# Attention beside a paged decode: key sums one step later behind GpSimd's products, a fifth key buffer, and the queries' low part on all 128 rows

## The chip, the cores and the metric

The kernel runs on one core of one Trainium2 chip. The core has a matrix engine (TensorE, PE in the profile, with its weight loads as PEld), three engines for elementwise work (VectorE as DVE, ScalarE as ACT, GpSimd as POOL), and a queue that issues the transfers (SyncE, SP or SPq). The metric is the device time of one execution in microseconds; the median of several runs counts.

## The reference

One inference step of a two-layer trunk runs for a prompt of 1024 tokens and for 8 samples of one token each, with a past of 4096 tokens in pages. The first layer holds stick-breaking attention (8 heads of 64) beside a pooling branch; the second is a convolution module. Cut to what the change touches:

```python
def stick_breaking(q, k, v, q_pos, k_pos, sb_bias):
    z = jnp.einsum('bqhd,bkhd->bhqk', q, k) / math.sqrt(SB_HEAD_DIM) + sb_bias[None, :, None, None]
    causal = k_pos[None, :] < q_pos[:, None]
    log_keep = jnp.where(causal, jax.nn.log_sigmoid(-z), 0.0)
    after = lax.cumsum(log_keep, axis=3, reverse=True) - log_keep
    w = jnp.where(causal, jnp.exp(jax.nn.log_sigmoid(z) + after), 0.0)
    return jnp.einsum('bhqk,bkhd->bqhd', w, v)

# the pooling branch, windows w of 2, 4, 8 and 16 tokens, one per group of 128 columns
        diffs.append((hi - lo) / count[None, :, None] - uf[:, POOL_STATE:, c0:c1])
    y = jnp.einsum('btgc,gcd->btgd', jnp.stack(diffs, axis=2), w_pool) * pool_scale
```

For the samples, q has one row and k and v are 4096 past rows, gathered by a page table. All values are float32. The kernel splits each operand of a large product into a high part that the matrix engine takes in its float32r format and a low part, the rest, and sums the partial products.

## The kernel before

The program is written in one order, and each engine and the DMA queue keep the order in which their instructions are written. The first layer's projection is cut into blocks of 128 output columns, each over three chunks of 384, 384 and 264 tokens. A generator, `blocks_gen`, writes it piece by piece (24 matmuls per chunk, L225 to L227), so that attention can be written between the pieces. Weights arrive as `wraw`; ACT writes the high part `whi` (L205), GpSimd the low part `wlo` (L210).

Attention runs over 48 units: four pairs of heads, eight query blocks of 128 rows, and for query blocks 4 to 7 two pieces of keys. Per pair there are thus four units of 256 columns (the widths 128 and 256, padded to 256), two of 384 and six of 512. For a unit, `z_a` writes the scores into two PSUM tiles, one per head: a full-array matmul each from the queries' high part `sq` (tile qh) and the keys `km`, then a matmul each on 64 rows from the low part `ql`, and, in a query block's first piece, a mask through identb and maskb (L823). `stick_a` forms the two sigmoids on ACT (L360, L361), `z_b` the running product by a scan (L365) and the weights `sg` (L369, L371) on DVE. `tpart` transposes the weights one unit later (L845), and `ppart` multiplies them with the values (L861). `prep` makes the two query parts for the next 256 query rows, in 16 calls: ACT copies the high part, DVE subtracts for the low part (L794), and copies on the DMA queue put each head's high part on both halves of the rows (L796, and L797 two points later).

Beside this runs `decode_k`, the samples' scores. Attention lets it make a certain number of steps per unit (`tick`), 2.3 to 3.8 by its width. In each step it loads two pages of keys into a buffer of 512 KB (`kt`, tag kv, L405), multiplies the pages loaded two steps earlier with the query row (L417; 7 of 8 on GpSimd, the eighth on DVE), and sums a product over the 64 columns of each head on DVE (L409). The steps left over when attention ends go one by one into the output projection's groups (L1029 to L1031), in which DVE also makes some weights' low parts.

The pooling branch, `evac_u`, takes a chunk of the projection out of PSUM: ACT copies it to `u`, DVE forms the window sum in `cur` (L694 or the scan L697) and from it `hb` (L705). Later `g2` multiplies hb with a weight (L713), scales it, gates it on GpSimd (L715) and stores it.

Of the kernel before, what the change touches and what calls it, by code (L numbers as in the profile page):

```python
# [14 lines left out]
F32 = mybir.dt.float32  # L15
# [49 lines left out]
KBUF = 4  # L65
# [35 lines left out]
def kernel(  # L101
# [75 lines left out]
    def defer(n, fn):  # L177
        deferred.append([n, fn])
# [210 lines left out]
    def decode_k():  # L389
        qrow = {0: query_rows(0)}  # L390
        yield
        for hf in range(2):
# [5 lines left out]
            for s in range(len(units) + KLAG + 1):  # L398
                if s < len(units):
                    bi, j = units[s]  # L400
                    if j % 4 == 0:
                        pg = page_ids(hf * 4 + bi, j, 4)
                    kt = dk.tile([P, 2, HW], F32, tag="kv", name="kt", bufs=KBUF)
                    for i in range(2):
                        sp.dma_start(kt[:, i, :], ck[ds(pg[j % 4 + i], 1)].rearrange("o t f -> t (o f)"))  # L405
                    kts[s] = kt
                if s >= KLAG + 1:
                    bi, j = units[s - KLAG - 1]
                    dve.tensor_reduce(out=seg[:, j // 8, j % 8:j % 8 + 2, bi * 8:bi * 8 + 8],  # L409
                                      in_=kts.pop(s - KLAG - 1).rearrange("p a (h d) -> p a h d", d=DH),  # L410
                                      op=ALU.add, axis=AX.X)
                if KLAG <= s < len(units) + KLAG:
                    bi, j = units[s - KLAG]
                    b = hf * 4 + bi
                    kt = kts[s - KLAG]
                    eng = gp if (j // 2) % KMOD < KPOOL else dve
                    eng.tensor_tensor(out=kt, in0=kt, in1=qrow[b], op=ALU.mult)  # L417
                    if j == NPG - 6 and b < NB - 1:
                        qrow[b + 1] = query_rows(b + 1)
                yield  # L420
# [255 lines left out]
    def evac_u(g):  # L676
# [3 lines left out]
        def f(c, c0, n, o):  # L680
# [11 lines left out]
            cur = ab.tile([P, 16 + CMAX], F32, tag="us", name="us", bufs=2)  # L692
            if g == 0:
                dve.tensor_tensor(out=cur[:, 16:16 + m], in0=o[:, 0:m], in1=u[:, 15:15 + m], op=ALU.add)  # L694
            else:
                prev = state["cur"][:, 15 + CMAX:16 + CMAX] if c else 0.0
                dve.tensor_tensor_scan(out=cur[:, 16:16 + m], data0=o[:, 0:m], data1=u[:, 16 - w:16 + m - w],  # L697
                                       initial=prev, op0=ALU.add, op1=ALU.subtract)
            state["cur"] = cur
            hb = ab.tile([P, CMAX], F32, tag="hbt", name="hbt", bufs=2)  # L700
            if c == 2:
                dve.tensor_tensor(out=cur[:, 16 + m:16 + n], in0=o[:, m:n], in1=spool[:, g, :],
                                  op=ALU.add)
            s0 = 0 if c else w - 1
            dve.scalar_tensor_tensor(out=hb[:, s0:n], in0=cur[:, 16 + s0:16 + n], scalar=1.0 / w,  # L705
                                     in1=o[:, s0:n], op0=ALU.mult, op1=ALU.subtract)
            if c == 0:
                gp.tensor_tensor(out=hb[:, 0:w - 1], in0=cur[:, 16:16 + w - 1], in1=rcnt[:, 0:w - 1], op=ALU.mult)
# [80 lines left out]
    def prep(pair, i):  # L789
        q = QO[:, pair, i * 256:(i + 1) * 256]  # L790
        sq = ab.tile([P, 2, 256], F32R, tag="qh", name="qh", bufs=2)
        ql = ab.tile([P, 256], F32R, tag="ql", name="ql", bufs=2)
        act.activation(out=sq[:, 0], in_=q, func=AF.Copy)
        dve.tensor_tensor(out=ql, in0=q, in1=sq[:, 0].bitcast(F32), op=ALU.subtract)  # L794
        for r in (slice(0, DH), slice(DH, P)):
            sp.dma_start(sq[r, 1].bitcast(F32), sq[DH:P, 0].bitcast(F32))  # L796
        defer(2, lambda: sp.dma_start(sq[DH:P, 0].bitcast(F32), sq[0:DH, 0].bitcast(F32)))  # L797
        SQ[pair, i] = sq, ql
# [7 lines left out]
    def z_a(u):  # L806
# [4 lines left out]
        sq, ql = SQ[pair, qb // 2]  # L811
# [4 lines left out]
        for hh in range(2):  # L816
            r = slice(hh * DH, hh * DH + DH)
            pe.matmul(zs[hh][:, 0:nz], ql[r, qs], km[r, hh, c0:c0 + nz], start=False, stop=not first)
# [865 lines left out]
```

## Time and profile before

| | |
|---|---|
| median of 3 runs | 1142.12 us (1140.06 to 1147.91) |
| the profiled execution | 1143.3 us |
| its span in the profile | 1141.5 us |
| PE, PEld busy | 1051.7 us (92%), 841.7 us (74%) |
| DVE, ACT, POOL busy | 812.6 us (71%), 491.9 us (43%), 665.1 us (58%) |
| granted TensorE clock, mean | 0.971 |

The profile's span is 1.8 us shorter than the execution's own time. The busy shares are means over stages with different limits; attention lies between about 70 and 500 us.

### The profile page before, as it was taken

The page shows a single profiled execution, that of the slowest core. Times are in us where ns is not written, and L with a number is a line of the kernel's source. Part 1 is how long each engine was busy: PE and PEld are TensorE (multiplying, and loading weights), DVE is VectorE, ACT ScalarE, POOL GpSimd, SP SyncE. Part 2 cuts the span into 40 slices and gives each one's busy share as a digit, 9 for nine tenths or more (in the row PEclk, how much of TensorE's full clock was granted, in tenths as well). Part 3 has the DMA queues.
Part 4 walks back from the last instruction along what each step waited for, and adds up shares of the span by engine and source line. Part 5 has one row for each costly group of instructions (what it writes and reads, how often), then busy time and mean ns, then how long its engine had stood idle before and what let it go on. Part 6 is the DMA issues. An engine that isn't in the chain of part 4 may idle for free.

```text
span 1141.5 us, 19830 instructions
## 1 busy us (share of the span) xinstructions
PE 1051.7 (92%) x6804; PEld 841.7 (74%) x6804; DVE 812.6 (71%) x961; ACT 491.9 (43%) x929; POOL 665.1 (58%) x502
## 2 busy tenths in 40 slices
PE   8998888889999998797998999999999999899994
PEld 7897777768877877697997666566666466677784
DVE  3458878688599898767348399999999960484246
ACT  4345465547565565571204224444544422462210
POOL 3277879691788889872418336765766612343235
PEclk9999999999999999898999999999999999899997
DMA  8577767783467976655203887787687678386922
GB/s 267 170 230 231 243 194 222 207 251 98 141 217 219 278 216 216 199 194 203 68 26 142 240 253 249 234 252 217 194 266 236 210 237 264 122 280 218 322 102 113
DMA packets 179206, 235.20 MB, mean 206 GB/s; under 512 B 15418, under 2 KB 95939, under 8 KB 179081
## 3 DMA queue, kind: packets, MB, share of 16 engines
q1 hardware_dynamic: 179105, 233.94, 65.1%
q8 instruction: 53, 0.87, 0.3%
q14 instruction: 48, 0.39, 0.1%
HBM read 212.60 MB, written 16.14 MB: 200 GB/s over the span
## 4 chain that ended last, share of the span: by engine, by line
PE 54%; POOL 13%; DVE 11%; issue 9%; DMA 7%; ACT 3%; SPq 3%; POOLq 0%; DVEq 0%; ACTq 0%
PE acc L225 11%; PE acc L227 10%; PE acc L226 10%; POOL kt L417 7%; PE qv L1151 5%; DMA kt<-in_cache_k_dram 3%; DVE zw L409 3%; PE acc L1029 3%; POOL wlo L210 2%; PE acc L1031 2%; PE acc L1030 2%; DVE kp L365 2%; DMA vt<-in_cache_v_dram 1%; DVE xl L196 1%; POOL xres L1021 1%
## 5 line engine op out<-in xcount | busy, mean ns | idle before, releaser
L225 PE MATMUL acc<-xh,whi 128*128 128x384 f32 (+2 forms) x960 | 361.5, 377 | 11.5 <-DVE hbt L705 5.7
L227 PE MATMUL acc<-xl,whi 128*128 128x384 f32 (+2 forms) x960 | 340.4, 355 | 0.2 <-DVE xl L196 0.2
L226 PE MATMUL acc<-xh,wlo 128*128 128x384 f32 (+2 forms) x960 | 339.7, 354 | 0.0
L417 POOL TENSOR_TENSOR kt<-kt,qbs 128x1024 f32<-128x1024 f32 x112 | 274.1, 2464 | 39.6 <-DMA kt<-in_cache_k_dram 30.0
L210 POOL TENSOR_TENSOR wlo<-wraw,whi 128x512 fp32r<-128x512 f32 x122 | 161.6, 1328 | 184.1 <-ACT whi L205 179.5
L1373 DVE SCALAR_TENSOR_TENSOR conv_acc<-hbuf,wdwT,conv_acc 128x1024 f32<-128x1024 f32 x196 | 252.8, 1290 | 6.8
L225 PEld LDWEIGHTS acc<-xh,whi 128*128 128x128 f32 x960 | 184.3, 192 | 78.1 <-issue 26.1
L409 DVE TENSOR_REDUCE zw<-kt 128x16 f32<-128x1024 f32 x128 | 153.6, 1212 | 63.5 <-POOL kt L417 63.3
L227 PEld LDWEIGHTS acc<-xl,whi 128*128 128x128 f32 x960 | 184.3, 192 | 18.0 <-DVE xl L196 0.7
L226 PEld LDWEIGHTS acc<-xh,wlo 128*128 128x128 f32 x960 | 185.0, 193 | 15.7 <-issue 0.3
L1363 POOL TENSOR_TENSOR conv<-conv,tap 128x512 f32<-128x512 f32 x84 | 105.9, 1293 | 17.6 <-ACT tap L1360 17.6
L1029 PE MATMUL acc<-whi,xh 128*128 128x256 f32 x352 | 102.4, 291 | 0.0
L1031 PE MATMUL acc<-whi,xl 128*128 128x256 f32 x352 | 99.5, 283 | 2.1 <-DVE xl L196 2.1
L1030 PE MATMUL acc<-wlo,xh 128*128 128x256 f32 x352 | 99.4, 282 | 0.0
L365 DVE TENSOR_TENSOR_SCAN kp<-kp,zt 128x512 f32<-128x512 f32 (+3 forms) x96 | 92.4, 963 | 1.2 <-ACT zt L361 1.2
L205 ACT ACTIVATE whi<-wraw 128x512 fp32r<-128x512 f32 x126 | 77.4, 624 | 32.1 <-DMA wraw<-in_w_out_ab_dram 14.1
L360 ACT ACTIVATE kp<-zt,nbiash 128x512 f32<-128x512 f32 (+3 forms) x96 | 55.8, 581 | 71.4 <-DVE sg L371 40.7
L1360 ACT ACTIVATE tap<-hbuf,wdwT 128x512 f32<-128x512 f32 x84 | 59.7, 721 | 48.0 <-POOL conv L1363 38.1
L1151 PE MATMUL qv<-vt,zw 128*32 128x512 f32 x512 | 76.1, 604 | 3.1 <-DMA vt<-in_cache_v_dram 3.1
L1029 PEld LDWEIGHTS acc<-whi,xh 128*128 128x128 f32 x352 | 66.8, 190 | 7.9 <-issue 7.4
L1031 PEld LDWEIGHTS acc<-whi,xl 128*128 128x128 f32 x352 | 67.0, 190 | 2.3 <-DVE xl L196 2.3
L845 PE MATMUL zt<-ident,sg 128*128 128x128 f32 x288 | 44.7, 286 | 24.2 <-DVE sg L371 12.9
(274 smaller groups left out, 1507.3 us busy)
## 6 DMA issues: line engine op xcount, KB each, us to landing
kt<-in_cache_k_dram SPq DMA_DIRECT2D x256, 256.0 KB
vt<-in_cache_v_dram SPq DMA_DIRECT2D x256, 256.0 KB
wraw<-in_w_in_c_dram SPq DMA_DIRECT2D x48, 256.0 KB
vt<-in_w_in_c_dram SPq DMA_DIRECT2D x48, 256.0 KB
wraw<-in_w_in_ab_dram SPq DMA_DIRECT2D x46, 256.0 KB
xt<-in_x_prompt_dram SPq DMA_DIRECT2D x8, 512.0 KB
wraw<-in_w_out_ab_dram SPq DMA_DIRECT2D x16, 256.0 KB
xres<-in_x_prompt_dram SPq DMA_DIRECT2D x8, 512.0 KB
```

What stands on the lines that cost most here:

```text
L210: (eng or gp).tensor_tensor(out=lo, in0=raw, in1=hi.bitcast(F32), op=ALU.subtract)
L225: pe.matmul(o, hi[:, k % 4, :], xh, start=(k == 0), stop=False)
L226: pe.matmul(o, lo[:, k % 4, :], xh, start=False, stop=False)
L227: pe.matmul(o, hi[:, k % 4, :], xl, start=False, stop=(k == NK - 1))
L365: dve.tensor_tensor_scan(out=kr, data0=kr, data1=z[:, 0:1].broadcast_to([P, n]), initial=1.0 if prev is None else prev, op0=ALU.mult, op1= ...
L409: dve.tensor_reduce(out=seg[:, j // 8, j % 8:j % 8 + 2, bi * 8:bi * 8 + 8], in_=kts.pop(s - KLAG - 1).rearrange("p a (h d) -> p a h d", d=DH),
L417: eng.tensor_tensor(out=kt, in0=kt, in1=qrow[b], op=ALU.mult)
L1029: pe.matmul(o, XH[:, k, cs], hi[:, k % 2, :], start=(k == 0), stop=False)
L1030: pe.matmul(o, XH[:, k, cs], lo[:, k % 2, :], start=False, stop=False)
L1031: pe.matmul(o, XL[:, k, cs], hi[:, k % 2, :], start=False, stop=(k == NK - 1))
L1151: pe.matmul(pv[32 * bi:32 * bi + 32, :], Z[:, j % 8 * 4 + j // 8, :], vts[bi], start=(j == 0), stop=(j == NPG - 1), tile_position=(0, 32 * ...
L1373: dve.scalar_tensor_tensor(out=part[1], in0=hb[:, j:j + S], scalar=w, in1=part[1], op0=ALU.mult, op1=ALU.add)
```

## The change

The number of key buffers goes from four to five, and a key sum stands two steps behind its product instead of one. The low part of the queries gets a second plane (`sl`) and is copied to both halves of the rows as the high part is, so that its score matmuls take 128 rows, and the four matmuls of a unit alternate between the two PSUM tiles in pairs. The window sum of the pooling branch is written into hb directly; the tile `us` shrinks to the one column that the next chunk's scan starts from.

```diff
--- before.py
+++ after.py
@@ -62,7 +62,7 @@
 TAT = 2
 WLEAD = 2
 G2LAG = 5
-KBUF = 4
+KBUF = 5
 WRB = 3
 ETICK = 0.35
 EDVE = (1, 2, 3, 0)
@@ -395,7 +395,7 @@
             seg = Z.rearrange("p (g s) r -> p s g r", s=4)
             units = [(bi, j) for bi in range(4) for j in range(0, NPG, 2)]
             kts = {}
-            for s in range(len(units) + KLAG + 1):
+            for s in range(len(units) + KLAG + 2):
                 if s < len(units):
                     bi, j = units[s]
                     if j % 4 == 0:
@@ -404,10 +404,10 @@
                     for i in range(2):
                         sp.dma_start(kt[:, i, :], ck[ds(pg[j % 4 + i], 1)].rearrange("o t f -> t (o f)"))
                     kts[s] = kt
-                if s >= KLAG + 1:
-                    bi, j = units[s - KLAG - 1]
+                if s >= KLAG + 2:
+                    bi, j = units[s - KLAG - 2]
                     dve.tensor_reduce(out=seg[:, j // 8, j % 8:j % 8 + 2, bi * 8:bi * 8 + 8],
-                                      in_=kts.pop(s - KLAG - 1).rearrange("p a (h d) -> p a h d", d=DH),
+                                      in_=kts.pop(s - KLAG - 2).rearrange("p a (h d) -> p a h d", d=DH),
                                       op=ALU.add, axis=AX.X)
                 if KLAG <= s < len(units) + KLAG:
                     bi, j = units[s - KLAG]
@@ -689,23 +689,23 @@
                 act.activation(out=u[:, 0:16], in_=state["u"][:, CMAX:16 + CMAX], func=AF.Copy)
             state["u"] = u
             act.activation(out=u[:, 16:16 + n], in_=o, func=AF.Copy)
-            cur = ab.tile([P, 16 + CMAX], F32, tag="us", name="us", bufs=2)
+            hb = ab.tile([P, CMAX], F32, tag="hbt", name="hbt", bufs=2)
             if g == 0:
-                dve.tensor_tensor(out=cur[:, 16:16 + m], in0=o[:, 0:m], in1=u[:, 15:15 + m], op=ALU.add)
+                dve.tensor_tensor(out=hb[:, 0:m], in0=o[:, 0:m], in1=u[:, 15:15 + m], op=ALU.add)
             else:
-                prev = state["cur"][:, 15 + CMAX:16 + CMAX] if c else 0.0
-                dve.tensor_tensor_scan(out=cur[:, 16:16 + m], data0=o[:, 0:m], data1=u[:, 16 - w:16 + m - w],
+                prev = state["cur"] if c else 0.0
+                dve.tensor_tensor_scan(out=hb[:, 0:m], data0=o[:, 0:m], data1=u[:, 16 - w:16 + m - w],
                                        initial=prev, op0=ALU.add, op1=ALU.subtract)
-            state["cur"] = cur
-            hb = ab.tile([P, CMAX], F32, tag="hbt", name="hbt", bufs=2)
+                if c < 2:
+                    state["cur"] = ab.tile([P, 1], F32, tag="us", name="us", bufs=2)
+                    dve.tensor_copy(state["cur"], hb[:, m - 1:m])
             if c == 2:
-                dve.tensor_tensor(out=cur[:, 16 + m:16 + n], in0=o[:, m:n], in1=spool[:, g, :],
-                                  op=ALU.add)
+                dve.tensor_tensor(out=hb[:, m:n], in0=o[:, m:n], in1=spool[:, g, :], op=ALU.add)
             s0 = 0 if c else w - 1
-            dve.scalar_tensor_tensor(out=hb[:, s0:n], in0=cur[:, 16 + s0:16 + n], scalar=1.0 / w,
+            dve.scalar_tensor_tensor(out=hb[:, s0:n], in0=hb[:, s0:n], scalar=1.0 / w,
                                      in1=o[:, s0:n], op0=ALU.mult, op1=ALU.subtract)
             if c == 0:
-                gp.tensor_tensor(out=hb[:, 0:w - 1], in0=cur[:, 16:16 + w - 1], in1=rcnt[:, 0:w - 1], op=ALU.mult)
+                gp.tensor_tensor(out=hb[:, 0:w - 1], in0=hb[:, 0:w - 1], in1=rcnt[:, 0:w - 1], op=ALU.mult)
                 gp.tensor_tensor(out=hb[:, 0:w - 1], in0=hb[:, 0:w - 1], in1=u[:, 16:16 + w - 1], op=ALU.subtract)
 
             def g2():
@@ -789,13 +789,18 @@
     def prep(pair, i):
         q = QO[:, pair, i * 256:(i + 1) * 256]
         sq = ab.tile([P, 2, 256], F32R, tag="qh", name="qh", bufs=2)
-        ql = ab.tile([P, 256], F32R, tag="ql", name="ql", bufs=2)
+        sl = ab.tile([P, 2, 256], F32R, tag="ql", name="ql", bufs=2)
         act.activation(out=sq[:, 0], in_=q, func=AF.Copy)
-        dve.tensor_tensor(out=ql, in0=q, in1=sq[:, 0].bitcast(F32), op=ALU.subtract)
-        for r in (slice(0, DH), slice(DH, P)):
-            sp.dma_start(sq[r, 1].bitcast(F32), sq[DH:P, 0].bitcast(F32))
-        defer(2, lambda: sp.dma_start(sq[DH:P, 0].bitcast(F32), sq[0:DH, 0].bitcast(F32)))
-        SQ[pair, i] = sq, ql
+        dve.tensor_tensor(out=sl[:, 0], in0=q, in1=sq[:, 0].bitcast(F32), op=ALU.subtract)
+        for t in (sq, sl):
+            for r in (slice(0, DH), slice(DH, P)):
+                sp.dma_start(t[r, 1].bitcast(F32), t[DH:P, 0].bitcast(F32))
+
+        def dup():
+            for t in (sq, sl):
+                sp.dma_start(t[DH:P, 0].bitcast(F32), t[0:DH, 0].bitcast(F32))
+        defer(2, dup)
+        SQ[pair, i] = sq, sl
 
     chs = []
     for u, x in enumerate(units):
@@ -808,14 +813,12 @@
         n = c1 - c0
         nz = max(n, 256)
         km = KT[pair]
-        sq, ql = SQ[pair, qb // 2]
+        sq, sl = SQ[pair, qb // 2]
         qs = slice(qb % 2 * P, qb % 2 * P + P)
         zs = [trp(), trp()]
         for hh in range(2):
             pe.matmul(zs[hh][:, 0:nz], sq[:, hh, qs], km[:, hh, c0:c0 + nz], start=True, stop=False)
-        for hh in range(2):
-            r = slice(hh * DH, hh * DH + DH)
-            pe.matmul(zs[hh][:, 0:nz], ql[r, qs], km[r, hh, c0:c0 + nz], start=False, stop=not first)
+            pe.matmul(zs[hh][:, 0:nz], sl[:, hh, qs], km[:, hh, c0:c0 + nz], start=False, stop=not first)
         sk = []
         for hh in range(2):
             h = pair * 2 + hh
```

On DVE, where the second half of the samples begins (sg: attention weights, zw<-kt: a key sum, ql: the queries' low part), there stands before:

```order
L369 TENSOR_TENSOR sg<-zt,kp 128x256
L409 TENSOR_REDUCE zw<-kt 128x2x8
L794 TENSOR_TENSOR ql<-qo,qh 128x256
L409 TENSOR_REDUCE zw<-kt 128x2x8 x2
L365 SCALAR_TENSOR_TENSOR kp<-kp,zt 128x384
L369 TENSOR_TENSOR sg<-zt,kp 128x384
L365 SCALAR_TENSOR_TENSOR kp<-kp,zt 128x384
L369 TENSOR_TENSOR sg<-zt,kp 128x384
L409 TENSOR_REDUCE zw<-kt 128x2x8 x2
L365 SCALAR_TENSOR_TENSOR kp<-kp,zt 128x512
```

and now:

```order
L369 TENSOR_TENSOR sg<-zt,kp 128x256
L794 TENSOR_TENSOR ql<-qo,qh 128x256
L409 TENSOR_REDUCE zw<-kt 128x2x8
L365 SCALAR_TENSOR_TENSOR kp<-kp,zt 128x384
L369 TENSOR_TENSOR sg<-zt,kp 128x384
L365 SCALAR_TENSOR_TENSOR kp<-kp,zt 128x384
L369 TENSOR_TENSOR sg<-zt,kp 128x384
L409 TENSOR_REDUCE zw<-kt 128x2x8 x2
L365 SCALAR_TENSOR_TENSOR kp<-kp,zt 128x512
```

By this place three key sums stood ahead of the scans over 384 columns; now it is one, since each sum has moved back a step and the first half ended a step later.

On the DMA queue, at a preparation in the first pair (qh and ql: the query parts, wraw: a weight, kt: key pages, km and kl: the keys' parts, ISA: an address from the page table), before:

```order
L796 DMA qh<-qh 64x256 x2
L200 DMA wraw<-in_w_in_ab_dram 128x4x128
L352 TENSOR_LOAD pt
L405 ISA
L405 DMA kt<-in_cache_k_dram 128x512
L405 ISA
L405 DMA kt<-in_cache_k_dram 128x512
L612 DMA km<-km 64x384
L613 DMA km<-kl 64x384
L797 DMA qh<-qh 64x256
```

and now:

```order
L797 DMA qh<-qh 64x256 x2
L797 DMA ql<-ql 64x256 x2
L200 DMA wraw<-in_w_in_ab_dram 128x4x128
L352 TENSOR_LOAD pt
L405 ISA
L405 DMA kt<-in_cache_k_dram 128x512
L405 ISA
L405 DMA kt<-in_cache_k_dram 128x512
L612 DMA km<-km 64x384
L613 DMA km<-kl 64x384
L801 DMA qh<-qh 64x256
L801 DMA ql<-ql 64x256
```

Three copies of the low part are added, two of them ahead of a weight and the next key pages.

On DVE, where the output projection begins (xres<-xres,zt or acc: a group taken out of PSUM, wlo: a weight's low part), before:

```order
L1062 SCALAR_TENSOR_TENSOR xres<-xres,zt 128x256
L1066 BN_STATS st<-xres 128x6
L409 TENSOR_REDUCE zw<-kt 128x2x8
L417 TENSOR_TENSOR kt<-kt,qbs 128x1024
L1062 SCALAR_TENSOR_TENSOR xres<-xres,zt 128x256
L1066 BN_STATS st<-xres 128x6
L409 TENSOR_REDUCE zw<-kt 128x2x8
L210 TENSOR_TENSOR wlo<-wraw,whi 128x512
L1062 SCALAR_TENSOR_TENSOR xres<-xres,acc 128x256
L1066 BN_STATS st<-xres 128x6
```

and now:

```order
L1065 SCALAR_TENSOR_TENSOR xres<-xres,zt 128x256
L1069 BN_STATS st<-xres 128x6
L409 TENSOR_REDUCE zw<-kt 128x2x8
L1065 SCALAR_TENSOR_TENSOR xres<-xres,zt 128x256
L1069 BN_STATS st<-xres 128x6
L409 TENSOR_REDUCE zw<-kt 128x2x8
L417 TENSOR_TENSOR kt<-kt,qbs 128x1024
L210 TENSOR_TENSOR wlo<-wraw,whi 128x512
L1065 SCALAR_TENSOR_TENSOR xres<-xres,acc 128x256
L1069 BN_STATS st<-xres 128x6
L409 TENSOR_REDUCE zw<-kt 128x2x8
L1065 SCALAR_TENSOR_TENSOR xres<-xres,zt 128x256
```

The last product on DVE has moved directly ahead of a weight's low part, and key sums follow in groups that had none.

## Rows read from the trace of the kernel before

**Rows 1.** Stretches view, 70 to 500 us: busy us per engine, granted clock, DMA.
```profile
70.00:500.00 430.00, 383.92 (x2621) 333.13 (x2621) 342.63 (x416) 241.41 (x503) 335.85 (x185) 0.96 0.69 211
```

**Rows 2.** Waits of PE from 55 to 530 us: total us, times, longest.
```profile
PE zt L845 <- DVE sg L371: 12.9, 7, 3.2
PE zt L845 <- DVE sg L369: 10.8, 10, 2.4
PE acc L225 <- DVE hbt L705: 5.7, 4, 2.3
PE acc L225 <- DVE kl L611: 5.5, 2, 3.4
```

**Rows 3.** Waits of DVE from 55 to 530 us.
```profile
DVE zw L409 <- POOL kt L417: 63.3, 33, 5.4
```

**Rows 4.** Groups by line, 70 to 500 us: the products and the key sums.
```profile
L417 POOL TENSOR_TENSOR kt<-kt,qbs 128x1024 f32<-128x1024 f32 x107 | 261.7, 2463 | 39.6 <-DMA kt<-in_cache_k_dram 30.0 <-DVE kp L365 3.9 <-DVE zw L409 3.2
L409 DVE TENSOR_REDUCE zw<-kt 128x16 f32<-128x1024 f32 x122 | 146.5, 1212 | 60.5 <-POOL kt L417 60.2
```

**Rows 5.** Waits of the DMA queue (SPq), 60 to 500 us.
```profile
SPq L405 <- DVE zw L409: 71.9, 48, 6.3
```

**Rows 6.** Timeline of DVE: key sums at the first and the last place.
```profile
101.09 1.22 DVE L409 TENSOR_REDUCE zw<-kt 128x16 f32<-128x1024 f32 x1 [2.21 <-POOL kt L417]
...
466.91 1.22 DVE L409 TENSOR_REDUCE zw<-kt 128x16 f32<-128x1024 f32 x1 [0.67 <-POOL kt L417]
```

**Rows 7.** Timeline of PE just behind those two places.
```profile
107.20 0.66 PE L845 MATMUL zt<-ident,sg 128*128 128x128 f32 x4 [1.19 <-DVE sg L369]
...
472.47 0.77 PE L815 MATMUL zt<-km,qh 128*128 128x512 f32 x1 [4.89 <-DVE sg L371]
```

**Rows 8.** Stretches view, the first and the last slow-clock stretch.
```profile
120.00:130.00 10.00, 5.42 (x29) 4.24 (x27) 8.71 (x10) 3.39 (x8) 8.59 (x5) 0.83 0.76 244
440.00:450.00 10.00, 8.83 (x57) 8.06 (x58) 9.35 (x12) 7.60 (x14) 8.37 (x6) 0.83 0.62 200
```

**Rows 9.** Timeline of PE: two score groups and what follows each.
```profile
153.35 0.62 PE L815 MATMUL zt<-km,qh 128*128 128x512 f32 x2
153.90 0.50 PE L818 MATMUL zt<-km,ql 64*128 64x512 f32 x2
154.34 0.28 PE L823 MATMUL zt<-maskb,identb 128*128 128x128 bf16 x2
...
211.99 0.40 PE L815 MATMUL zt<-km,qh 128*128 128x256 f32 x2
212.63 0.28 PE L823 MATMUL zt<-maskb,identb 128*128 128x128 bf16 x2
```

**Rows 10.** Timeline of PE: full-array matmuls in a stream, 264 and 512 columns.
```profile
208.06 0.28 PE L226 MATMUL acc<-xh,wlo 128*128 128x264 f32 x1
208.18 0.28 PE L227 MATMUL acc<-xl,whi 128*128 128x264 f32 x1
...
751.23 0.40 PE L226 MATMUL acc<-xh,wlo 128*128 128x512 f32 x1
751.46 0.39 PE L227 MATMUL acc<-xl,whi 128*128 128x512 f32 x1
```

**Rows 11.** Tile view of qh: the copies and the subtraction, ns.
```profile
L796 SPq DMA_DIRECT2D qh<-qh x32: 465/566/1539, 60.8 to 416.1; - x32
L794 DVE TENSOR_TENSOR ql<-qo,qh x16: 415/590/2312, 59.5 to 422.9; 128x256 fp32r<-128x256 f32 x16
```

**Rows 12.** Timeline of DVE and PE where the output projection begins.
```profile
524.78 1.22 DVE L417 TENSOR_TENSOR kt<-kt,qbs 128x1024 f32<-128x1024 f32 x1
...
528.56 0.39 PE L1030 MATMUL zt<-wlo,xh 128*128 128x256 f32 x1 [2.62 <-DVE wlo L210]
```

**Rows 13.** Timeline of POOL and PE: a weight's low part and its use.
```profile
189.78 1.27 POOL L210 TENSOR_TENSOR wlo<-wraw,whi 128x512 fp32r<-128x512 f32 x1
...
191.28 0.34 PE L226 MATMUL acc<-xh,wlo 128*128 128x384 f32 x1
```

## The prediction

> **What bounds the kernel now.** I began with the stretches view over the attention stage, 70 to 500 us, since every edit lies in that stage or in the first groups behind it [rows 1]. The reader is to see that TensorE is busy 383.9 of 430 us, so 46 us are idle, and that DVE is busy 342.6. Next came TensorE's waits [rows 2]: the four groups shown are 34.9 us of them, and all four end with DVE. Then DVE's own waits [rows 3]: 33 times, 63.3 us in all, the key sum (L409) stood at the head of DVE's queue until GpSimd had finished its product (L417). Busy time and these waits together fill DVE's stretch to some 94% ((342.6 + 60.2) / 430, [rows 1, 4]); DVE looks 80% busy, but the scans behind a key sum find it nearly full. GpSimd is not full: 335.9 of 430 us, and it stands 30.0 us for key loads [rows 1, 4]. Those loads in turn stood 71.9 us in the DMA queue for a key sum to free a buffer [rows 5]. So sum, load, product and sum again make a loop through four buffers, in which each engine waits for the other, and TensorE pays where DVE comes late.
>
> How much TensorE pays I took from two timelines laid side by side. At 13 places an idle gap of TensorE with DVE as its releaser comes within 7 us behind a key sum that waited; counting each place at the smaller of its wait and its gap gives 23.7 us. The first place counts 1.2 us (a wait of 2.21, a gap of 1.19), the last 0.7 (a wait of 0.67, a gap of 4.89) [rows 6, 7].
>
> **The key sums and the fifth buffer.** A key sum moves one scheduling step back, so that two steps lie between a product and its sum; 122 sums in 430 us make a step 3.5 us [rows 4]. A load still follows the sum that frees its buffer by one step, but now that sum belongs to a product three steps old, not two. A wait is 1.9 us in the mean and 5.4 at most (63.3 / 33, [rows 3]), so one step covers nearly every wait that stands alone. Where waits follow each other within a few steps they add up, and one step is all that is given. The ends are 0 (GpSimd keeps falling behind and the waits move one step) and 23.7 us; I take two thirds, 16 us, nearer the upper end because GpSimd has 22% to spare and 30 us of its idle time is the loop itself [rows 1, 4].
>
> The clock belongs to the same gaps. Behind such a gap the granted clock falls: five stretches of 10 us at about 0.83, the first at 120 and the last at 440 us [rows 8], each costing some 1.7 us of full-speed work. If all went, 8.5 us; in proportion to the gaps taken, 5.7; I take 5 (bounds 0 and 8.5).
>
> The price lies at the stage's end. Two steps more (one for each half of the samples) put two more key sums into the first output groups, and the order shows DVE's last product directly ahead of a weight's low part (L210) for which TensorE already waits 2.62 us. That product takes 1.22 us [rows 12]. The two sums (1.21 us each, [rows 4]) come where DVE soon idles 3.5 us in any case. Between 1.2 and 3.6 us are lost; I take 2.
>
> **The scores.** Before, two full-array matmuls are followed by two on 64 rows each. The latter two are issued together and the next instruction follows 0.44 us after them, so they do overlap; but the step from the second full matmul to them is longer than a stream's, since the pair of full ones and the wait behind it takes 0.55 us [rows 9] where two of 512 columns take 0.46 in a stream (0.23 each, [rows 10]). After, four full matmuls run as a stream. With the mask behind them (32 of the 48 units) it goes as follows.
> - 256 columns, 16 units: 0.64 us before [rows 9], 4 x 0.12 = 0.48 after [rows 10]: 16 x 0.16 = 2.6 us gained.
> - 512 columns, 8 units: 0.99 before, 0.92 after: 0.6 us gained. The 8 units of 384 columns lie between, some 0.9.
> - The 16 units of 512 columns without a mask are followed by output matmuls on half the columns. I let the long step (0.55 - 0.23 = 0.32 us) fall there: 3 x 0.23 + 0.32 = 1.01 after, 0.99 before, 0.3 us lost.
>
> That is 3.8 us gained; if the step to the bf16 mask costs 0.1 us where the one to the 64-row pair did, 3.2 of it go. I take 2 (bounds 0.5 and 3.8). In "TensorEngine Tiling (Array Packing)", section Key Properties, the Trainium skill says that tiles work in parallel but that changing the tiling mode drains the engine. By its first half alone the scores would cost 8.9 us more, as a rival below works out from rows, and the sum would end at -6; by its second they gain. The trace agrees with both halves: the pair overlaps, and the steps to it and from it are long.
>
> **The doubled low part.** Each of 16 preparations issues three more copies of 64 KB. One issue holds the DMA queue for 0.57 us in the median [rows 11], so 27 us of that queue in all, and two of the three stand behind DVE's subtraction (L794), which takes up to 2.3 us. Behind them in that queue are a weight load and the next key loads. What hides this: a key load has two steps, 7 us, until its product, and the scores that need the copies come two units or more later. I take 1 us; the upper end is the slow rival below.
>
> **The pool branch.** The window sum now goes straight into hb; six one-column copies are added, and the first DVE instruction of a chunk, not the second, waits for hb to be free. TensorE already waits 5.7 us for that branch [rows 2]. Nothing below zero is likely, as the long instructions stay; I take 1 us (0 to 3).
>
> **A new wait.** If DVE and TensorE run earlier against GpSimd, a weight's low part can come too late. At one place it ends at 191.05 and its matmul starts at 191.28 [rows 13]; a step there would cost up to 3.5 us. I take 2.
>
> **The sum.** -16 - 5 - 2 + 2 + 1 + 1 + 2 = -17 us. The profiled execution took 1143.3 us (its span 1141.5, and 1.8 around it); that makes 1126.3. The median of the runs shown is 1142.1, 1.2 lower, so the forecast is 1125 us. All terms at their best give -34.8, 1107; its own range is 1110 to 1133.
>
> **The rivals.**
> - GpSimd sets the pace: the sums stop waiting, but low parts, memsets and pool products queue behind the key products and TensorE waits for these. For it: it is busy 84 to 86% of some stretches [rows 8]. Against it: 30 us of its idle time belongs to the loop. Gaps -8, clock -2, scores -2, costs +6: 1136.
> - The change doesn't do what it says: the waits are one step longer than the slack each time, and only the costs are seen: 1142 - 2 + 4 = 1144. Against it speaks the mean wait of 1.9 us.
> - The packed pair was cheaper than I read: a second pass costs its full stream time, 24 x 0.23 + 8 x 0.18 + 16 x 0.12 = 8.9 us, in place of the 2 gained: 1136. Against it: the 0.44 us behind an overlapped pair [rows 9].
> - Slower: the DMA queue. If the copies' 1.6 us of issues and a subtraction 2.3 us late hold back the next key load each time, GpSimd has one product (2.46 us, [rows 4]) to bridge 3.9, and 16 x 1.4 = 23 us reach DVE and TensorE, with nothing gained: 1165. It decides from the point at which a load lands after GpSimd has run out of products, as it does already for 30 us.
>
> **How the numbers follow.** The chances: forecast 0.54, GpSimd 0.20, no effect 0.12, packed pair 0.05, DMA queue 0.09. One per cent is 11.4 us, about what a measurement here can tell from no change, so faster is under 1130.7 and slower over 1153.5. Nine tenths of the forecast and a quarter of the GpSimd case are faster: 0.53. The DMA case is slower: 0.09. The rest, 0.38, is within 1%. The range runs from 1111 to 1143: nearly all of the forecast, the GpSimd and packed cases whole, and half of the case without effect.
>
> **What would show it.** In the profile after, DVE's wait of L409 for L417 should fall from 63 to about 20 us, GpSimd's wait for key loads from 30 to under 15, TensorE's busy share between 70 and 500 us should rise above 92%, and the stage should end 15 to 20 us earlier, with fewer stretches at a reduced clock. The score groups should be four matmuls some 0.12 us apart at 256 columns. TensorE waiting for L210 would show the GpSimd case; key loads waiting for the subtraction, the DMA case. I am wrong if the key-sum waits fall and TensorE's gaps stay, or if the waits stay.

## The result, and the profile after

| | before | after |
|---|---|---|
| median | 1142.31 us (1139.52 to 1149.19, 20 runs) | 1149.47 us (1145.09 to 1155.51, 20 runs) |
| the profiled execution | 1143.3 us | 1145.09 us |
| its span in the profile | 1141.5 us | 1143.3 us |

The ratio is 1.0057, with a 95% interval of 1.004 to 1.0074: the change makes the kernel 7.2 us slower, where 17 us less were forecast. The profiled execution of the changed kernel is the lowest of its 20, 4.4 us under their median, so its trace shows less than the whole loss.

The stretches view over 70 to 500 us of the changed kernel answers to [rows 1] (busy us of PE, PEld, DVE, ACT and POOL, then the granted clock, DMA share, GB/s):

```profile
70.00:500.00 430.00, 384.59 (x2628) 341.36 (x2627) 346.25 (x420) 239.58 (x502) 328.68 (x182) 0.96 0.71 216
```

TensorE is busy 384.6 of 430 us, 89%, as before; over 92% were forecast. The waits from 55 to 530 us answer to [rows 2, 3, 5]: PE's first, then DVE's, POOL's and the DMA queue's (total us, times, longest).

```profile
PE zt L848 <- DVE sg L369: 10.1, 13, 1.9
PE zt L848 <- DVE sg L371: 8.9, 8, 2.3
PE acc L225 <- DVE hbt L705: 6.3, 3, 3.5
PE zt L820 <- DMA qh<-qh: 5.8, 3, 3.2
...
DVE zw L409 <- POOL kt L417: 37.5, 24, 4.5
...
POOL kt L417 <- DMA kt<-in_cache_k_dram: 46.8, 22, 6.1
...
SPq L405 <- DVE zw L409: 43.3, 23, 3.7
...
SPq L797 <- DVE ql L794: 11.1, 8, 2.9
```

The loop of sum, load and product did loosen: the key sums wait 37.5 us for GpSimd in place of 63.3, and the queue waits 43.3 us for a key sum in place of 71.9. But GpSimd stands 46.8 us for key loads in place of 30.0. For the subtraction the queue now stands 11.1 us, 8 times, and TensorE waits 5.8 us for a copy of the queries' high part. Before, a copy stood for the subtraction once, the third one, which overwrites rows that the subtraction reads, and TensorE had no such wait:

```profile
SPq L797 <- DVE ql L794: 3.3, 1, 3.3
```

The chain of waits inside 70 to 500 us tells the same. GpSimd's product and the key loads have changed places in its shares by line. Before:

```profile
by line: POOL kt L417 17.7%; issue 13.5%; DMA kt<-in_cache_k_dram 7.7%; PE acc L225 7.3%; PE acc L226 6.4%; PE acc L227 6.4%; DVE zw L409 6.1%; DVE kp L365 5.8%; POOL wlo L210 3.5%; PE o L861 3.2%; PE zt L845 3.1%; DVE sg L369 2.0%; DVE kt 
```

And after:

```profile
by line: DMA kt<-in_cache_k_dram 17.5%; DVE kp L365 9.4%; issue 8.6%; DVE zw L409 8.1%; POOL kt L417 7.3%; PE acc L225 4.2%; SPq L405 4.0%; PE acc L226 3.7%; PE acc L227 3.7%; DVE sg L369 3.1%; DVE kt L417 2.9%; DMA wraw<-in_w_out_ab_dram 2
```

Behind the stage, from 493 to 643 us, TensorE's waits answer to [rows 12]:

```profile
PE zt L1033 <- DVE wlo L210: 7.5, 2, 4.9
...
PE acc L225 <- ACT sga_t L754: 2.2, 1, 2.2
```

In this execution the last attention output ended at 493.9 us, 1.9 us earlier than before (495.8), and the samples' first product with the values (L1154, before L1151) started at 642.7 us, 3.4 us later (639.3). So 5.3 us were lost between the two. The waits for a weight's low part, 1.4 us longer (7.5 in place of 6.1), and a new one of 2.2 us are 3.6 of them.

**One preparation, followed through the queues.** The timeline of SP in the changed kernel, at the preparation of 172 us (start us, duration us; the address instructions are not shown):

```profile
172.51 1.12 SPq L797 DMA_DIRECT2D qh<-qh  x2
174.81 0.34 SPq L716 DMA_DIRECT2D hb_dram<-hbt  x1
177.43 1.10 SPq L797 DMA_DIRECT2D ql<-ql  x2
179.09 1.98 SPq L405 DMA_DIRECT2D kt<-in_cache_k_dram  x4
181.11 0.43 SPq L200 DMA_DIRECT2D wraw<-in_w_in_ab_dram  x1
181.58 0.51 SPq L801 DMA_DIRECT2D qh<-qh  x1
```

DVE's, POOL's and PE's timelines there:

```profile
175.22 2.17 DVE L794 TENSOR_TENSOR ql<-qo,qh 128x256 fp32r<-128x256 f32 x1
...
182.70 2.38 POOL L417 TENSOR_TENSOR kt<-kt,qbs 128x1024 f32<-128x1024 f32 x1 [4.15 <-DMA kt<-in_cache_k_dram]
...
187.43 0.69 PE L820 MATMUL zt<-km,qh 128*128 128x384 f32 x1 [3.21 <-DMA qh<-qh]
```

The subtraction ends at 177.39 us, and the two copies of the low part go out at 177.43. Four key loads come only behind them, 6.6 us after the high part's copies (172.51 to 179.09), and GpSimd then stands 4.15 us. The third copy of the high part is behind these loads in turn, and TensorE stands 3.21 us for it. In the kernel with the key sums' part alone (the first experiment below), the same place on SP reads:

```profile
168.79 1.11 SPq L796 DMA_DIRECT2D qh<-qh  x2
171.48 0.34 SPq L716 DMA_DIRECT2D hb_dram<-hbt  x1
172.77 3.32 SPq L405 DMA_DIRECT2D kt<-in_cache_k_dram  x4
176.13 0.43 SPq L200 DMA_DIRECT2D wraw<-in_w_in_ab_dram  x1
176.67 0.48 SPq L797 DMA_DIRECT2D qh<-qh  x1
```

Here the loads follow 4.0 us after the copies, and the third copy starts 7.9 us behind the first in place of 9.1.

### The profile page after: what moved, and what is told of

Same layout as the page of the kernel before. It is cut to its first block, busy times and chain, and to the rows that moved or that the text cites. A ratio compares the mean times of both kernels' runs of the same rounds, so it can differ in the third digit from the quotient of the medians.

```text
span 1143.3 us, 19899 instructions
## 1 busy us (share of the span) xinstructions
PE 1049.0 (92%) x6804; PEld 848.3 (74%) x6804; DVE 818.9 (72%) x967; ACT 490.7 (43%) x929; POOL 663.8 (58%) x502
## 4 chain that ended last, share of the span: by engine, by line
PE 50%; DVE 14%; DMA 12%; POOL 8%; issue 6%; SPq 5%; ACT 4%; POOLq 0%; DVEq 0%; ACTq 0%
PE acc L225 10%; PE acc L227 9%; PE acc L226 9%; DMA kt<-in_cache_k_dram 7%; PE qv L1154 5%; DVE kp L365 4%; DVE zw L409 3%; POOL kt L417 3%; PE acc L1032 3%; PE acc L1034 2%; PE acc L1033 2%; DMA vt<-in_cache_v_dram 2%; PE qv L1190 2%; SPq L405 2%; DVE xl L196 1%
## 5 line engine op out<-in xcount | busy, mean ns | idle before, releaser
L417 POOL TENSOR_TENSOR kt<-kt,qbs 128x1024 f32<-128x1024 f32 x112 | 269.2, 2420 | 57.8 <-DMA kt<-in_cache_k_dram 46.8
L409 DVE TENSOR_REDUCE zw<-kt 128x16 f32<-128x1024 f32 x128 | 152.7, 1211 | 37.6 <-POOL kt L417 37.5
L1154 PE MATMUL qv<-vt,zw 128*32 128x512 f32 x512 | 74.4, 600 | 3.7 <-DMA vt<-in_cache_v_dram 3.5
L1033 PEld LDWEIGHTS acc<-wlo,xh 128*128 128x128 f32 x352 | 66.3, 188 | 1.2 <-POOL wlo L210 1.2
```

The source lines that it names most:

```text
L1033: pe.matmul(o, XH[:, k, cs], lo[:, k % 2, :], start=False, stop=False)
L1154: pe.matmul(pv[32 * bi:32 * bi + 32, :], Z[:, j % 8 * 4 + j // 8, :], vts[bi], start=(j == 0), stop=(j == NPG - 1), tile_position=(0, 32 * ...
```

## The experiments

Two theories stood after the result. One: the new copies cost the whole gain, by their issues on the DMA queue ahead of the key loads. The other: the key sums' step gave nothing, because waits only moved to another place, or the full-array matmuls cost what a second pass costs. Each kernel below was timed beside the kernel before, whose median was 1143.13 us for the first four kernels, 1143.45 for the next four and 1142.42 for the last four. Waits and timelines are those of one execution of each kernel, and that one is often not the median: it has the highest time of its kernel for the sums alone (1128.39 us) and the issues without the wait (1143.18), the lowest for the fifth buffer alone (1134.98). Small differences between such traces say little.

### The key sums alone

The fifth buffer, the sum two steps behind, and the pooling branch (which makes room for the buffer); the queries' low part as before.

```diff
-KBUF = 4
+KBUF = 5
...
-                if s >= KLAG + 1:
-                    bi, j = units[s - KLAG - 1]
+                if s >= KLAG + 2:
+                    bi, j = units[s - KLAG - 2]
...
-            cur = ab.tile([P, 16 + CMAX], F32, tag="us", name="us", bufs=2)
+            hb = ab.tile([P, CMAX], F32, tag="hbt", name="hbt", bufs=2)
```

> The change without its doubled low part: fifth buffer, key sums two steps behind, pool branch in hb (which makes room for the buffer). Theory A (the loss is the doubled part's copies in the DMA queue, which hold back key loads): about 1132 us, ratio 0.991, and GpSimd's wait for key loads back to 30 us or less. Rival B (the later sums themselves buy nothing, since a load still leads its product by two steps, and they cost at the stage's end): 1146 us or more, ratio 1.003 to 1.006, GpSimd's wait for loads 40 us or more.

Measured: 1125.94 us, ratio 0.9852 (0.9828 to 0.9877). Its stretch of 70 to 500 us, and its waits from 55 to 530 us:

```profile
70.00:500.00 430.00, 399.11 (x2741) 348.77 (x2740) 357.34 (x435) 252.50 (x525) 341.51 (x190) 0.96 0.69 216
```

```profile
PE zt L845 <- DVE sg L369: 7.7, 10, 1.4
PE zt L845 <- DVE sg L371: 4.8, 5, 1.4
...
DVE zw L409 <- POOL kt L417: 22.9, 17, 4.0
...
POOL kt L417 <- DMA kt<-in_cache_k_dram: 20.9, 13, 4.0
```

TensorE is busy 399.1 us, 93%, and its two waits for the weights `sg` fell from 23.7 to 12.5 us. The mechanism is there and is worth 17.2 us, some 6 us more than the first theory expected. The theory that the waits only move is refuted.

### The doubled low part alone

The kernel before with `sl`, its three copies and the four full-array matmuls; four buffers, sums one step behind.

```diff
-        ql = ab.tile([P, 256], F32R, tag="ql", name="ql", bufs=2)
+        sl = ab.tile([P, 2, 256], F32R, tag="ql", name="ql", bufs=2)
...
-            pe.matmul(zs[hh][:, 0:nz], ql[r, qs], km[r, hh, c0:c0 + nz], start=False, stop=not first)
+            pe.matmul(zs[hh][:, 0:nz], sl[:, hh, qs], km[:, hh, c0:c0 + nz], start=False, stop=not first)
```

> The kernel before with the doubled low part alone: three more copies per preparation and four full-array score matmuls. Theory A: slower, 1150 to 1158 us, ratio 1.007 to 1.014. Rival B: no loss, 1139 to 1143, ratio 0.997 to 1.001. If the packed pair was cheaper than read, 1150 without a longer wait for key loads.

Measured: 1167.88 us, ratio 1.0225 (1.02 to 1.0249), 24.7 us more. Its waits from 55 to 530 us:

```profile
DVE zw L409 <- POOL kt L417: 77.9, 38, 5.6
...
POOL kt L417 <- DMA kt<-in_cache_k_dram: 64.1, 30, 6.9
...
SPq L797 <- DVE ql L794: 20.0, 8, 7.3
```

The chain is seen link by link: the queue waits 20.0 us for the subtraction, GpSimd 64.1 for loads (30.0 before), the sums 77.9 for GpSimd (63.3 before), and TensorE 31.4 for the weights `sg` (23.7 before). The loss is 10 us more than the first theory's upper bound.

### The pooling branch alone

```diff
-                dve.tensor_tensor(out=cur[:, 16:16 + m], in0=o[:, 0:m], in1=u[:, 15:15 + m], op=ALU.add)
+                dve.tensor_tensor(out=hb[:, 0:m], in0=o[:, 0:m], in1=u[:, 15:15 + m], op=ALU.add)
```

> The kernel before with the pool branch written into hb, nothing else. All theories: within 0.2%, 1140 to 1145 us. If the branch is the loss, 1147 or more, and TensorE's wait for hbt (L705) well over 6 us.

Measured: 1143.39 us, ratio 0.9999 (0.9982 to 1.0017). It costs nothing that can be measured.

### The whole change with later copies

The low part's first two copies (`spread`) go out two points later, the third (`dup`) four points later.

```diff
-        defer(2, dup)
+        spread(sq)
+        defer(2, lambda: (dup(sq), spread(sl)))
+        defer(4, lambda: dup(sl))
```

> The whole change, with the low part's first two copies issued two points later (with the late copy of the high part) and its third four points later, so that the DMA queue no longer stands for DVE's subtraction. Theory A, if the standing is what costs: 1135 to 1142 us, the waits of L797 for the subtraction near 0. If the copies' issue time costs, still 1146 to 1150. Rival B: 1147 to 1150.

Measured: 1142.04 us, ratio 0.9996 (0.9979 to 1.0013), 7.4 us less than the whole change, 16.1 more than the sums alone. One of TensorE's waits from 55 to 530 us is new:

```profile
PE zt L822 <- DMA ql<-ql: 20.2, 6, 4.9
```

The queue stands only 0.6 us for the subtraction (11.1 with the whole change), but now the scores stand for the copies. So this kernel can't say how much the issues cost by themselves; the next ones were made for that.

### The copies without the full-array matmuls

The whole change, but the low matmuls take 64 rows of the copied planes.

```diff
-            pe.matmul(zs[hh][:, 0:nz], sl[:, hh, qs], km[:, hh, c0:c0 + nz], start=False, stop=not first)
+        for hh in range(2):
+            r = slice(hh * DH, hh * DH + DH)
+            pe.matmul(zs[hh][:, 0:nz], sl[r, hh, qs], km[r, hh, c0:c0 + nz], start=False, stop=not first)
```

> The whole change with its six copies per preparation, but the low part's score matmuls on 64 rows as before. Theory A (the copies in the DMA queue are the loss): as the whole change, 1146 to 1153 us, GpSimd's wait for key loads over 40 us. If the full-array matmuls are the loss: as the sums alone, 1124 to 1128.

Measured: 1148.46 us, ratio 1.0042 (1.0022 to 1.0061), 22.5 us more than the sums alone. GpSimd stands 48.2 us for key loads (20.9 with the sums alone), and TensorE 6.3 us for a copy of the queries' high part (0.7); it has no wait for a copy of the low part. The copies alone bring the whole loss.

### The full-array matmuls without the copies

The sums alone, and the second matmul of each head takes the high part on 128 rows once more. No copy is added; the low part's product is left out.

```diff
-            pe.matmul(zs[hh][:, 0:nz], ql[r, qs], km[r, hh, c0:c0 + nz], start=False, stop=not first)
+            pe.matmul(zs[hh][:, 0:nz], sq[:, hh, qs], km[:, hh, c0:c0 + nz], start=False, stop=not first)
```

> The sums alone with full-array matmuls for the second score product, and no new copy. It leaves out the low part: the queries' high part stands in its place. Theory A: 1122 to 1127 us, a gain of 0 to 4 over the sums alone (1125.9), as the prediction's rows of the score groups have it. If the packed pair was cheaper than read: 1130 to 1136.

Measured: 1125.53 us, ratio 0.9834 (0.9813 to 0.9855). That is 0.4 us under the sums alone by the medians and 0.0018 by the ratios, 2 us; the intervals overlap. So no cost of the matmuls is seen, and what they may gain isn't told from none.

### The issues without the wait for the subtraction

As the copies without the full-array matmuls, with as many issues of as many bytes. But the three new ones copy the high part into a plane that is not read, and so stand for ACT's copy, as the old ones do.

```diff
-                sp.dma_start(t[r, 1].bitcast(F32), t[DH:P, 0].bitcast(F32))
+                sp.dma_start(t[r, 1].bitcast(F32), sq[DH:P, 0].bitcast(F32))
...
+            sp.dma_start(sl[DH:P, 1].bitcast(F32), sq[0:DH, 0].bitcast(F32))
```

> The copies with the same number of issues and bytes, but the three new ones take the queries' high part into a plane that no one reads, so that they wait for ACT's copy as the old ones do and not for DVE's subtraction; score matmuls on 64 rows. If issue time or the copies' traffic is the loss: 1143 to 1152 us. If standing for the subtraction is: 1126 to 1133. Both share it if it lies between.

Measured: 1139.74 us, ratio 0.9968 (0.9955 to 0.998), 13.8 us more than the sums alone and 8.7 less than the copies that wait for DVE: both share in the loss. GpSimd's wait for key loads is 35.4 us, between 20.9 and 48.2, and the queue stands only 0.3 us for a new copy to land.

### The fifth buffer alone

The fifth buffer and the pooling branch; the sum stays one step behind.

```diff
-                if s >= KLAG + 2:
-                    bi, j = units[s - KLAG - 2]
+                if s >= KLAG + 1:
+                    bi, j = units[s - KLAG - 1]
```

(The first lines are those of the key sums alone.)

> The fifth key buffer and the pool branch, with key sums one step behind their product as before. If the gain of the sums alone comes from the room that a load has, it stays: 1126 to 1133 us. If it comes from DVE no longer standing for GpSimd: 1138 to 1143, DVE's wait of L409 for L417 still over 50 us.

Measured: 1138.11 us, ratio 0.9955 (0.9938 to 0.9971). Waits of DVE and POOL from 55 to 530 us:

```profile
DVE zw L409 <- POOL kt L417: 59.6, 32, 5.5
...
POOL kt L417 <- DMA kt<-in_cache_k_dram: 17.1, 12, 3.6
```

The buffer cuts GpSimd's wait for loads from 30.0 to 17.1 us, and yet brings only 5.3 us: DVE still stands 59.6 us at the sums. The other 12.2 us (1138.11 - 1125.94) come with the sum's step.

### Issues of 2 KB

As the issues without the wait, but the new copies carry 8 columns in place of 256.

```diff
+        for t, m in ((sq, 256), (sl, 8)):
...
+                sp.dma_start(t[r, 1, 0:m].bitcast(F32), sq[DH:P, 0, 0:m].bitcast(F32))
```

> As the run with the issues alone, but the three new copies per preparation take 8 columns in place of 256 (2 KB each in place of 64 KB). If the issues as such hold the DMA queue: 1136 to 1142 us, as with the full copies (1139.7). If the bytes in transfer are the cost: 1126 to 1130, as the sums alone.

Measured: 1138.51 us, ratio 0.9958 (0.9937 to 0.9978): as with 64 KB, 0.0010 less by the ratio, within the intervals. The new copies in the tile view of ql, ns (shortest, median, longest), are these here:

```profile
L797 SPq DMA_DIRECT2D ql<-qh x32: 461/587/595, 62.0 to 415.0; - x32
```

and in the kernel with 64 KB:

```profile
L797 SPq DMA_DIRECT2D ql<-qh x32: 540/587/1518, 62.5 to 422.2; - x32
```

The median issue is 587 ns either way, and GpSimd's wait for key loads is 35.3 us (35.4 with 64 KB). The cost is one of issues, not of bytes.

### The low part's copies on ACT's queue

The whole change, with the three copies of the low part issued by ACT, one and three points later.

```diff
+                act.dma_start(sl[r, 1].bitcast(F32), sl[DH:P, 0].bitcast(F32))
...
+        defer(1, spread)
         defer(2, dup)
+        defer(3, lambda: act.dma_start(sl[DH:P, 0].bitcast(F32), sl[0:DH, 0].bitcast(F32)))
```

> The whole change, the low part's three copies issued from ACT's queue one and three points later; the key loads' queue issues no more than before. Theory A (it is the order in one queue): 1122 to 1132 us, if ACT's own time for the issues and a wait of TensorE for late copies cost little. If the copies cost wherever they are issued (bytes, engines): 1140 to 1150.

Measured: 1146.53 us, ratio 1.0018 (0.9995 to 1.0041). Only 2.9 us return, where 17 or more were expected of the order in one queue. SP issues none of these copies, but by its waits from 55 to 530 us it stands for them to land, ahead of the high part's copies and of key loads:

```profile
SPq L796 <- DMA ql<-ql: 15.6, 5, 6.3
...
SPq L405 <- DMA ql<-ql: 7.1, 3, 3.8
```

In the traces of the whole change and of the copies without the full-array matmuls, where SP issues them, the queue has no such wait. So this kernel does not take the copies out of the key loads' way, and it doesn't decide between the two cases that were expected.

### Loads three steps ahead

Five buffers, loads three steps ahead of the product, the sum one step behind it.

```diff
-KLAG = 2
+KLAG = 3
```

(The sum's lines are those of the fifth buffer alone.)

> The fifth buffer given to the loads: key loads three steps ahead of their product, key sums one step behind it; pool branch as in the change. If loads are what the stage waits for: below the buffer alone (1138), 1128 to 1134 us, GpSimd's wait for loads under 15 us. If DVE's standing for GpSimd is: 1138 to 1144, that wait near 60 us still.

Measured: 1134.72 us, ratio 0.9919 (0.9893 to 0.9945). It lies between the two cases expected: GpSimd's wait for loads falls to 12.0 us, and DVE still stands 51.4 us at the sums. With the same five buffers, a step given to the load brings 7.7 us against the kernel before; given to the sum it brings 17.2.

### The sums alone with the old copies on ACT's queue

```diff
-            sp.dma_start(sq[r, 1].bitcast(F32), sq[DH:P, 0].bitcast(F32))
-        defer(2, lambda: sp.dma_start(sq[DH:P, 0].bitcast(F32), sq[0:DH, 0].bitcast(F32)))
+            act.dma_start(sq[r, 1].bitcast(F32), sq[DH:P, 0].bitcast(F32))
+        defer(2, lambda: act.dma_start(sq[DH:P, 0].bitcast(F32), sq[0:DH, 0].bitcast(F32)))
```

> The sums alone, with the old three copies of the high part issued from ACT's queue as well. Theory A says that these hold the key loads too: 1116 to 1124 us, GpSimd's wait for loads below the 20.9 us of the sums alone. If three copies were harmless and six too many: 1125 to 1128; if ACT's time for the issues costs more: over 1128.

Measured: 1145.59 us, ratio 1.003 (1.001 to 1.0049), 19.7 us more than with the same copies on SP's queue. ACT's timeline at one preparation:

```profile
138.00 0.42 ACT L793 ACTIVATE qh<-qo 128x256 fp32r<-128x256 f32 x1
138.45 2.44 ACTq L796 DMA_DIRECT2D qh<-qh  x2
141.00 0.63 ACT L205 ACTIVATE whi<-wraw 128x512 fp32r<-128x512 f32 x1 [2.58 <-issue]
```

and from the waits of ACT, SP and PE from 55 to 530 us:

```profile
ACT wt L847 <- DVE ql L794: 14.5, 4, 5.6
...
SPq L405 <- DMA qh<-qh: 20.0, 6, 5.4
...
PE zt L815 <- ACT wt L847: 17.0, 8, 3.1
```

ACT computes nothing for 2.58 us here while it issues two copies. This place is a long one; over all 32 such copies the median issue on ACT is 0.47 us:

```profile
L796 ACTq DMA_DIRECT2D qh<-qh x32: 467/471/1937, 59.6 to 421.9; - x32
```

ACT also stands 14.5 us for DVE's subtraction, ahead of the weights' copies out of PSUM (`wt`). The third copy, which must not overwrite the rows before the subtraction has read them, is now in ACT's own order. TensorE waits 17.0 us for `wt`. And the key loads on SP's queue stand 20.0 us for copies issued by ACT, so they are not free of them either. How much of the 19.7 us belongs to each was not separated.

The fastest version that leaves no work out is the key sums alone, 1125.94 us, 17.2 us under the kernel before and 23.5 under the changed one. Fewer issues for the same copies (one transfer for both planes) were not tried, nor was the whole change with loads three steps ahead.

## Why the prediction was wrong, point by point

**The step that failed** is "The doubled low part", sized at 1 us. It measured 22.5 us on top of the sums, and 24.7 on the kernel before. The issues were counted rightly: 48 of some 0.57 us, 27 us of queue time, two of three behind the subtraction [rows 11]; after, the median is 0.59. What was wrong is the cover: "a key load has two steps, 7 us, until its product". By the rows that lead was not in reserve. The queue stood 71.9 us for a sum to free a buffer [rows 5], so many a load went out only when a buffer came free, and GpSimd already stood 30.0 us for loads [rows 4]. The rows that proved loads late were read for the loop and not for the copies. No run gave the loads a longer lead together with the copies, so this reason is read from the waits and not tested by itself. The second cover, that "the scores that need the copies come two units or more later", failed too: the third copy of the high part went out behind the delayed loads, and TensorE stood 5.8 us for it in the changed kernel (0.7 with the sums alone). Of the 22.5 us, 13.8 come with the issues alone, 0.86 per preparation, half of the 1.7 us by which three issues hold the queue; 8.7, or 0.54 per preparation, come with standing for the subtraction, which held the queue 11.1 us, 0.7 per preparation.

**The slow rival had the path, and its price by luck.** GpSimd's wait for loads grew as it said, and "16 x 1.4 = 23 us" is near what the copies cost. But its working does not hold: it took 2.3 us for the subtraction each time, where the mean was 0.7, and one product of 2.46 us as cover. By its own rule the issues alone, 1.7 us per preparation, would have cost nothing, and they cost 13.8. Its time, 1165 us, failed because it took the copies' cost "with nothing gained". The gain of the sums and the cost of the copies are separate effects, and both came: each measured on the kernel before, 24.7 - 17.2 = 7.5 us, and 7.2 were measured. As rivals, each with the other at nothing, they could not add up; the loss of 0.6% lay between the cases and was given to none.

**The key sums** were right in mechanism and nearly in size. With them alone the last attention output ended at 480.3 us, 15.5 earlier than before, against 16 taken for the gaps. L409's wait fell to 22.9 ("about 20"), TensorE's share rose to 93% ("above 92%"); GpSimd's wait for loads, 20.9, stayed over the 15 named. That the sum's step matters more than the load's is shown by the fifth buffer alone (5.3 us) and the loads three steps ahead (7.7).

**The clock** (5 us taken) rose a little, but the traces don't show it. In them its mean in the stage is 0.96 in the kernel before, after and with the sums alone. Of the 43 stretches of 10 us, six lie under 0.9 before (the five of [rows 8] and one at 0.66 from 470 us that was not counted), seven with the sums alone, and nine after. But the profiled execution of the sums alone has the lowest clock of its six, 0.969; the other five have 0.973 to 0.980, and the mean of the six is 0.975. The 23 executions of the kernel before beside them have 0.963 to 0.974, in the mean 0.970, and the 20 of the changed kernel 0.970 too. What the rise of 0.005 is worth was not separated. Among the 23, a clock higher by 0.01 goes with about 4 us less, loosely (a correlation of 0.56), which makes it some 2 us, an estimate. After, the clock falls at the new gaps too; the stretch with the 3.21 us wait of above and the next one read:

```profile
180.00:190.00 10.00, 6.79 (x36) 5.61 (x35) 7.15 (x10) 2.22 (x7) 6.36 (x5) 0.85 0.85 252
190.00:200.00 10.00, 10.00 (x54) 9.30 (x55) 7.15 (x9) 6.05 (x14) 9.43 (x6) 0.81 0.80 248
```

Behind that wait matmuls of 384 columns stood 0.32 us apart (187.91 to 188.23), and ahead of it 0.18 (183.19 to 183.37): the granted level had fallen from 2.4 to 1.2 GHz.

The sum for the sums' part, -16 - 5 + 2 + 1 + 2 = -16 with tail, pool and new wait, hit -17.2 in part by luck: the clock's term was too large by that estimate, and the three costs were smaller than the 5 us taken.

**The scores** (2 us taken, bounds 0.5 and 3.8). Inside the groups it went as worked out. PE's timeline after, a group of 256 columns, answers to [rows 9]:

```profile
389.41 0.28 PE L820 MATMUL zt<-km,qh 128*128 128x256 f32 x1
389.52 0.28 PE L821 MATMUL zt<-km,ql 128*128 128x256 f32 x1
389.64 0.28 PE L820 MATMUL zt<-km,qh 128*128 128x256 f32 x1
389.76 0.28 PE L821 MATMUL zt<-km,ql 128*128 128x256 f32 x1
389.88 0.28 PE L826 MATMUL zt<-maskb,identb 128*128 128x128 bf16 x2
```

Four steps of 0.12 us: 0.47 us from the first to the mask, where it was 0.64. At the end the matmuls gave 0.4 to 2 us without the copies and cost 1.0 with them (1149.47 - 1148.46); neither can be told from nothing. The packed-pair rival, 8.9 us more for a second pass, is refuted. In the groups by line, 70 to 500 us, of the sums alone, the weight loads of the 64-row pair stand 10.7 us for nothing but their issue:

```profile
L818 PEld LDWEIGHTS zt<-km,ql 64*128 64x128 f32 x96 | 9.3, 191 | 12.8 <-issue 10.7
```

In the same view of the full-array matmuls without the copies, the second loads stand 0.8 us in all:

```profile
L816 PEld LDWEIGHTS zt<-km,qh 128*128 128x128 f32 x96 | 18.4, 192 | 0.8
```

The Trainium skill states in "TensorEngine Tiling (Array Packing)", section Key Properties, that a change of tiling mode drains TensorE. These rows agree with it: 10.7 us of standing are gone where the mode no longer changes. In the kernel's time that is not told from none.

**The pool branch** (1 us, 0 to 3) measured 0.3 with an interval on both sides of nothing. **The tail** (2 us, 1.2 to 3.6): after, 1.4 us more stand before the low part, 7.5 for 6.1 [rows 12]; with the sums alone these waits are 3.7 us, and a new one of 2.5 for GpSimd (crow) stands beside them. From the last attention output to the end the profiled executions take 645.7 us before and 646.3 with the sums alone, so 0.6 us were lost there. **The new wait** (2 us, 0 to 3.5) shows once with the sums alone, 1.2 us for a weight's low part from GpSimd. The GpSimd rival, 1136 us, is refuted by 1125.94 for the sums' part.

**What stays open.** The issues cost half of the queue time that they hold. A wait of the queue on their completion is not seen (0.3 us with 64 KB, none with 2 KB), but whether the copies also make key loads land later once these are issued was not separated. Some 5 us of the loss fall behind the stage: from the last attention output to the samples' first product with the values it is 148.8 us in the changed kernel and 143.9 with the sums alone (480.3 to 624.2). The waits named for the tail explain a part of that.

## What to carry to other kernels

A lead of so many steps covers a delay only if it is not used up already: where the trace shows the queue waiting for a buffer and the consumer waiting for the load, time that is put ahead of that load is paid, here about half of what the issues held. Count added transfers by their issues and by whom they stand for, not by bytes, and look what the same in-order queue carries behind them. And when one edit has a gain and another a cost, sum them as terms with their own ranges; a rival that sets the other edit to nothing hides the case in which both come true.

## What was not expected of the hardware

An issue of a copy between partitions holds the queue as long for 2 KB as for 64 KB, 587 ns in the median. On ACT's queue two such issues kept ACT from computing for 2.58 us at one place (the median issue there is 0.47 us). Moving three copies of each preparation to ACT cost 19.7 us, and SP's key loads stood 20.0 us for them all the same. In the profiled execution the granted clock's mean stayed at 0.96 when TensorE's idle time in the stage fell from 46 to 31 us; over all executions its mean rose from 0.970 to 0.975.
